# Two encoder layers on one core: where the second layer's weight sums are issued

## The chip, the cores and the metric

The kernel runs on one core of one Trainium2 chip. That core has a matrix engine (TensorE, PE in the profile; its weight loads are shown apart as PEld), three engines for element-wise work (VectorE is DVE, ScalarE is ACT, GpSimd is POOL), a queue that issues transfers (SyncE, SP) and 16 DMA engines, which move data between the chip's memory (DRAM) and the core's own. The metric is the time of one execution in microseconds (us), and the number given is the median of several runs. One further execution was recorded by the hardware profiler, and everything said of single instructions is from that one.

## The reference, cut to what matters

Two layers run over 512 tokens of width 1024, all in 32-bit floats. Each layer has a mixer (neighbourhood attention beside grouped-query attention, GQA), an attention over 256 memory tokens, and a feed-forward part:

```python
def conv_ffn(h, w_up, conv_w, conv_b, w_down):
    u = h @ w_up                                   # 512 x 1024 by 1024 x 5632
    up = jnp.pad(u, ((0, 0), (1, 1), (0, 0)))
    u = up[:, :-2] * conv_w[0] + up[:, 1:-1] * conv_w[1] + up[:, 2:] * conv_w[2] + conv_b
    gate, val = jnp.split(u, 2, axis=-1)
    return (jax.nn.silu(gate) * val) @ w_down      # 512 x 2816 by 2816 x 1024

for l in range(DEPTH):                             # DEPTH = 2
    x = x + hybrid_mixer(rms_norm(x, norm_mix[l]), w_in[l], ...)
    x = x + memory_cross_attention(rms_norm(x, norm_mem_q[l]), rms_norm(mem, norm_mem_kv[l]), ...)
    x = x + conv_ffn(rms_norm(x, norm_ffn[l]), w_up[l], conv_w[l], conv_b[l], w_down[l])
return rms_norm(x, norm_final)
```

## The kernel before, in words

The activations stand with the width on the 128 partitions, in 8 pieces of 128 x 512 (`xT`). The feed-forward width of 2816 is worked off in 22 columns of 128, `j` = 0 to 21, and for each column there is a gate half and a value half of the product with `w_up`.

**Weight sums.** Columns 0 to 3 (`PLAIN = 4`) are plain products (`up`). From column 4 on (`up_forms`, line 1975) the kernel cuts tokens, input width and gate/value into halves, and gets the eight half products of a column from seven, in the manner of Strassen and Winograd. Those seven need sums of weight blocks: from the four quarters of a `w_up` column (a11, a12 of the gate side, a21, a22 of the value side) the kernel makes two tensors in DRAM, `dr_sums` and `dr_diffs`. It makes them with transfers alone, no engine of the core adds anything. `make_form` (line 717) makes one half of one such tensor in two transfers: SP copies a quarter of `w_up` from DRAM to DRAM (shown as line 80), and then a transfer issued by POOL (line 731) adds a second quarter, or a sum made before, onto it. One call of `make_form` is called **a form** here. The columns 4 to 21 come in four shares (`SHARES_OF_FORMS`: columns 4 to 7, 8 to 11, 12 to 16, 17 to 21), each share needs four forms, so there are 16 forms in a layer. The transfers of a form carry 1024 KB each in the first two shares and 1280 KB in the last two.

The forms of both layers stand in one list, `form_queue`, the first layer's 16 ahead of the second layer's 16. Each call takes the next one from the list. The calls stand in the program at fixed places, the same in each layer:

- six in the GQA sweep (line 1737, at every third of its steps),
- four in the memory attention (line 1853),
- eleven in the feed-forward part (line 2173, at each even column: 0, 2, 4, ... 20).

That makes 21 places in a layer for 16 forms. `make_form(upto=DEPTH)` has an argument: it does nothing when the next form in the list belongs to a layer that is not below `upto`. In the kernel before, all three places call it without an argument.

**How the sums are read.** In the order of `sequence()` (line 848) each column from 4 on asks for four weight tiles, `gate`, `val` (of the column before), `sums` and `diffs`, and for tiles of `w_down` in between. SP loads each into one of five buffers named `raw` (`emit_raw`), ACT rounds it to `hi` (line 801), POOL, or DVE for the `sums`, subtracts to get the rest `lo` (line 802), and PE multiplies with both (line 103). After each product the partial results in the PSUM banks (`mm`, `sc`, `tr`) are put together by DVE, ACT and POOL (lines 2002 to 2051), and a bank is free for PE's next product only when that is done.

**What sets the order.** SP works strictly in the order in which the program is written: a load and a form's copy stand in one queue, and a load whose `raw` buffer is not yet free holds all that stands behind it. The order on PE, ACT, DVE and POOL comes from a planner in the kernel (`class Order`, line 359 on). It replays the whole program with a cost for each instruction and a model of the transfers, in 12 rounds with random draws, and keeps the best order that it finds. So a change to SP's queue can also move instructions on the other engines, even ahead of the place that was edited.

Of the kernel before, what the change touches and what calls it, by code (L numbers as in the profile page):

```python
# [695 lines left out]
def encoder_kernel(ctx: ExitStack, tc: tile.TileContext, t: dict, out: bass.AP):  # L696
# [20 lines left out]
    def make_form(upto=DEPTH):  # L717


        if not form_queue or form_queue[0][0] >= upto:  # L720
            return
        l, g, n = form_queue.pop(0)
        j, nj = SHARES_OF_FORMS[g]
        w, half = t["w_up"][l], D // 2
        gate, val = slice(P * j, P * (j + nj)), slice(D_FF + P * j, D_FF + P * (j + nj))
        sums, diffs = made[l][g]
        a11, a12, a21, a22 = w[:half, gate], w[half:, gate], w[:half, val], w[half:, val]
        dst, base, more = [(sums[:half], a21, a22), (sums[half:], a11, sums[:half]),
                           (diffs[half:], a11, a21), (diffs[:half], a12, sums[half:])][n]
        SP.dma_start(dst, base)  # L730
        nc.gpsimd.dma_start(dst, more, accum_op=ALU.add, max_dma_last_dim=4 * P * nj)
# [486 lines left out]
    for l in range(DEPTH):  # L1218
# [672 lines left out]
        def up(j):  # L1891
            up_finish(j, [up_project(j, side) for side in range(2)])
# [73 lines left out]
        def split_form(name, where=None):  # L1966


            place = xform[name] = [rtile((2, S)) for _ in range(2)] if where is None else [where[:, :2], where[:, 2:]]
            direct = {"b11": (0, 0), "b21": (1, 0), "b22": (1, 1)}  # L1970
            for i in range(len(place)):
                src = quarter(*direct[name])[i] if name in direct else raw_forms[name][:, 2 * i : 2 * i + 2]
                halves_of(name, i, src, name == "t4", POOL if name == "b22" else DVE)
# [81 lines left out]
        def down(g, rows):  # L2055
            j0, nj = GROUPS[g]
            ops = [acts[j] for j in range(j0, j0 + nj)]
            for m in rows:
                pm = ps_mm()
                gemm_T(pm, get_w(("down", g, m)), ops, range(nj), 0, nj - 1)  # L2060
                DVE.tensor_add(xT[m], xT[m], pm)
# [106 lines left out]
        for what, n, rows in sequence():  # L2168
            if what == "down":
                down(n, rows)  # L2170
                continue
            if what in ("up", "gate") and n % 2 == 0:
                make_form()
            if what == "gate":
                open_units[n] = up_forms(n)
            if what != "up":
                next(open_units[n])
                continue
            if n == 0:
                up_first()  # L2180
                token_sums()
            elif n > 1:
                up(n)
                if n == PLAIN - 1:
                    split_form("t3", ffn.hi[:, :4])
                    split_form("b22", ffn.lo[:, :4])
                    split_form("t4", ffn.hi[:, 4:])
# [92 lines left out]
```

## Time and profile before

| what | value |
|---|---|
| median of 3 runs | 1301.23 us (1299.8 to 1301.89) |
| the profiled execution: its time, its span | 1299.96 us, 1298.2 us |
| PE busy | 1286.4 us, 99% of the span |
| PEld, DVE, ACT, POOL busy | 84%, 71%, 61%, 66% |
| granted TensorE clock | 0.998 |
| data moved by DMA | 241.22 MB, mean 186 GB/s |

The span is the time from the first to the last instruction, and 1.76 us of the execution's time lie outside of it. "Busy" is the share of the span in which an engine had an instruction in work; PE's instructions overlap each other, so its busy time says that PE was hardly ever left without work, and not that it worked at its peak. In the rows of a timeline the columns are the start in us, the duration in us, the engine, the line of the program, the operation, what it writes and reads, and in square brackets how long the engine had been idle and who released it. In the rows of a tile the three numbers behind the count are the least, the median and the greatest duration in ns, and the two behind them the first and the last start in us. A row of DMA issues gives the count, the size of one transfer and the median us from issue to landing. In the rows of windows each engine has its busy us in that stretch and its number of instructions, and at the end stand the granted clock, the share of the time that the 16 DMA engines were busy, and GB/s.

### The profile page before, as it was taken

How to read it: one execution, taken by the hardware profiler on the slowest of the kernel's cores; microseconds unless marked ns; L12 is line 12 of the kernel's file. 1: busy time of each engine (PE TensorE's matmuls, PEld its weight loads, DVE VectorE, ACT ScalarE, POOL GpSimd, SP SyncE). 2: the span in 40 equal slices, each digit the busy share in tenths (PEclk: the TensorE clock that was granted, in tenths of full speed). 3: DMA queues.
4: the chain of work that ended last, by engine and by line, in shares of the span. 5: the costliest groups of instructions: out<-in, count | busy, mean ns of one | idle time of the engine just before them, and what ended most of it. 6: DMA issues, size and time to landing. Idle time of an engine off the chain costs nothing.

```text
span 1298.2 us, 19571 instructions
## 1 busy us (share of the span) xinstructions
PE 1286.4 (99%) x6731; PEld 1094.9 (84%) x6731; DVE 916.4 (71%) x1727; ACT 787.4 (61%) x1487; POOL 861.3 (66%) x656
## 2 busy tenths in 40 slices
PE   9999999999999999999999999999999999999997
PEld 8888888888888888888888888888888888888887
DVE  6558877668976765866635597776789767667565
ACT  6667867566554654554636678765656556456444
POOL 3657967727767776776746569767376776667663
PEclk9999999999999999999999999999999999999999
DMA  9734499596989898797455435998974555555541
GB/s 290 208 107 126 150 258 208 165 249 190 235 219 250 220 260 219 215 245 204 147 152 174 141 76 168 266 213 251 217 188 124 164 157 158 163 154 155 145 134 65
DMA packets 293699, 241.22 MB, mean 186 GB/s; under 512 B 7777, under 2 KB 249953, under 8 KB 293601
## 3 DMA queue, kind: packets, MB, share of 16 engines
q1 hardware_dynamic: 276288, 201.83, 52.4%
q0 software_dynamic: 16896, 37.75, 16.2%
q8 instruction: 53, 0.87, 0.3%
q10 hardware_dynamic: 416, 0.39, 0.1%
q14 instruction: 46, 0.37, 0.1%
HBM read 229.99 MB, written 77.59 MB: 237 GB/s over the span
## 4 chain that ended last, share of the span: by engine, by line
PE 94%; DVE 3%; ACT 1%; issue 1%; POOL 0%; POOLq 0%; ACTq 0%; DVEq 0%
PE mm L103 68%; PE sc L103 18%; PE tr L103 5%; PE tr L1606 2%; PE tr L1451 1%; PE tr L1800 1%; DVE sc L1423 0%; DVE r L1317 0%; DVE r L1100 0%; DVE t L1509 0%; ACT hi L801 0%; DVE r L1149 0%; PE tr L1521 0%; ACT t L1429 0%; DVE t L1476 0%
## 5 line engine op out<-in xcount | busy, mean ns | idle before, releaser
L802 POOL TENSOR_TENSOR lo<-raw,hi 128x512 fp32r<-128x512 f32 (+3 forms) x329 | 575.9, 1770 | 254.3 <-ACT hi L801 209.7
L801 ACT CAST hi<-raw 128x1024 fp32r<-128x1024 f32 (+2 forms) x369 | 295.0, 815 | 280.5 <-issue 60.1
L103 PE MATMUL mm<-r,hi 128*128 128x512 f32 (+1 forms) x1376 | 419.2, 389 | 0.0
L103 PEld LDWEIGHTS mm<-r,hi 128*128 128x128 f32 x1376 | 249.3, 188 | 43.8
L103 PE MATMUL mm<-r,lo 128*128 128x512 f32 (+1 forms) x864 | 261.4, 344 | 0.0
L103 PE MATMUL mm<-xg,hi 128*128 128x512 f32 x768 | 227.5, 392 | 1.3 <-DVE sc L2046 1.3
L103 PEld LDWEIGHTS mm<-r,lo 128*128 128x128 f32 x864 | 152.1, 188 | 26.8 <-DVE lo L802 1.7
L103 PEld LDWEIGHTS mm<-xg,hi 128*128 128x128 f32 x768 | 140.6, 188 | 28.1 <-ACT t L2031 1.5
L103 PE MATMUL mm<-xg,lo 128*128 128x256 f32 (+1 forms) x528 | 139.7, 331 | 0.0
L103 PE MATMUL mm<-hi,xg 128*128 128x512 f32 (+1 forms) x384 | 111.1, 359 | 0.0
L103 PEld LDWEIGHTS mm<-xg,lo 128*128 128x128 f32 x528 | 89.2, 188 | 15.4
L1106 POOL TENSOR_SCALAR t<-t,s 128x512 f32<-128x512 f32 (+1 forms) x112 | 67.7, 627 | 45.7 <-DVE s L1590 23.0
L103 PE MATMUL sc<-xg,hi 128*128 128x512 f32 x304 | 89.4, 395 | 0.0
L2044 POOL TENSOR_TENSOR t<-t 128x256 f32<-128x256 f32 x36 | 43.6, 1211 | 68.4 <-ACT t L2043 68.4
L103 PEld LDWEIGHTS mm<-hi,xg 128*128 128x128 f32 x384 | 68.0, 189 | 9.1 <-DVE r L1300 0.2
L802 DVE TENSOR_TENSOR lo<-raw,hi 128x1024 fp32r<-128x1024 f32 (+1 forms) x40 | 54.0, 1350 | 30.6 <-ACT hi L801 30.6
L103 PE MATMUL sc<-r,r 128*128 128x256 f32 (+1 forms) x352 | 73.9, 330 | 0.0
L103 PE MATMUL mm<-lo,xg 128*128 128x512 f32 (+1 forms) x192 | 68.5, 357 | 0.0
L1099 ACT CAST r<-tr 128x512 fp32r<-128x512 f32 x79 | 45.6, 587 | 36.4 <-DVE tr L1914 25.6
L2051 DVE TENSOR_TENSOR sc<-mm,t 128x256 f32<-128x256 f32 x36 | 15.6, 432 | 71.3 <-ACT t L2050 71.3
L103 PEld LDWEIGHTS sc<-xg,hi 128*128 128x128 f32 x304 | 55.6, 191 | 10.4 <-ACT xg L80 0.4
L1100 DVE TENSOR_TENSOR r<-tr,r 128x512 fp32r<-128x512 f32 x79 | 53.4, 685 | 12.4 <-ACT r L1099 8.8
(232 smaller groups left out, 2389.6 us busy)
## 6 DMA issues: line engine op xcount, KB each, us to landing
raw<-in_w_up SPq DMA_DIRECT2D x52, 512.0 KB, 4.8
raw<-dr_sums SPq DMA_DIRECT2D x36, 512.0 KB, 4.1
raw<-dr_diffs SPq DMA_DIRECT2D x36, 512.0 KB, 4.7
raw<-in_w_in SPq DMA_DIRECT2D x25, 512.0 KB, 5.0
raw<-in_w_down SPq DMA_DIRECT2D x32, 384.0 KB, 4.4
dr_sums<-in_w_up SPq DMA_DIRECT2D x8, 1280.0 KB, 9.9
dr_diffs<-in_w_up SPq DMA_DIRECT2D x8, 1280.0 KB, 9.2
raw<-in_w_up SPq DMA_DIRECT2D x36, 256.0 KB, 3.5
```

The source lines that it names most:

```text
L103: return self.engine.matmul(out, lhsT, rhs, **k)
L801: act.copy(hi[:, k], raw[:, k])
L802: (POOL if eng[0] == "P" else DVE).tensor_sub(lo[:, k], raw[:, k], f(hi)[:, k])
L1099: ACT.copy(hi, ps)
L1100: DVE.tensor_sub(lo, ps, f(hi))
L1106: eng.tensor_scalar(e, e, sums[:, col : col + 1], 1.0, op0=ALU.mult, op1=ALU.mult)
L1451: PE.transpose(tr[:, (2 * i + c) * P : (2 * i + c + 1) * P], es[j][:, i, c * P : (c + 1) * P], ident)
L1606: PE.transpose(tr[:, k * P : (k + 1) * P], es[j][:, k * P : (k + 1) * P], ident)
L1800: PE.transpose(tr[:, (2 * c + i) * P : (2 * c + i + 1) * P], e[:, i, c * P : (c + 1) * P], ident)
L2044: POOL.tensor_add(vc, vc, u2)
L2051: DVE.tensor_add(ch, ah, l4)
```

## The change

```diff
@@ -2170,7 +2170,7 @@
                 down(n, rows)
                 continue
             if what in ("up", "gate") and n % 2 == 0:
-                make_form()
+                make_form(l + 1)
             if what == "gate":
                 open_units[n] = up_forms(n)
             if what != "up":
```

`make_form` itself is as it was:

```python
    def make_form(upto=DEPTH):
        if not form_queue or form_queue[0][0] >= upto:
            return
        l, g, n = form_queue.pop(0)
        ...
        SP.dma_start(dst, base)
        nc.gpsimd.dma_start(dst, more, accum_op=ALU.add, max_dma_last_dim=4 * P * nj)
```

Only the calls in the feed-forward part are touched. In the first layer (`l` = 0) they now stop when the first layer's 16 forms are through. Ten of these are issued in the GQA sweep and the memory attention, six at the columns 0 to 10, and the calls at the columns 12 to 20 do nothing; before, those five issued the first five forms of the second layer. In the second layer the forms then begin with the first one of the layer: six in the GQA sweep, four in the memory attention, six at the columns 0 to 10. Before, the second layer had eleven forms left, and one of them fell into its feed-forward part. The number of transfers and of bytes over the whole program is the same.

SP's queue in the first layer's feed-forward part, at column 12. `dr_sums_86` is the second layer's first share (the number is the tile's), `raw` are the buffers into which weights are loaded. Before:

```order
L80 DMA raw_4918<-dr_diffs_83 128x8x128
L80 DMA raw_4946<-in_w_down 128x6x128
L80 DMA dr_sums_86<-in_w_up 512x512
L80 DMA raw_4979<-in_w_up 128x8x128
L80 DMA raw_5005<-in_w_up 128x4x128
L80 DMA raw_5035<-dr_sums_82 128x8x128
```

Now:

```order
L80 DMA raw_4918<-dr_diffs_83 128x8x128
L80 DMA raw_4946<-in_w_down 128x6x128
L80 DMA raw_4977<-in_w_up 128x8x128
L80 DMA raw_5003<-in_w_up 128x4x128
L80 DMA raw_5033<-dr_sums_82 128x8x128
```

The form's copy has gone from between the loads, and the loads stand in the order in which they stood.

SP's queue in the second layer's feed-forward part, at column 6. `dr_sums_86` is read here; `dr_sums_92` is the last share of the second layer, which is read from column 17 on. Before:

```order
L80 DMA raw_10512<-dr_sums_86 128x8x128
L80 DMA raw_10542<-in_w_down 128x5x128
L80 DMA raw_10566<-dr_diffs_87 128x8x128
L80 DMA raw_10594<-in_w_down 128x5x128
L80 DMA raw_10622<-in_w_up 128x8x128
L80 DMA raw_10648<-in_w_up 128x4x128
L80 DMA raw_10678<-dr_sums_86 128x8x128
```

Now:

```order
L80 DMA raw_10506<-dr_sums_86 128x8x128
L80 DMA raw_10536<-in_w_down 128x5x128
L80 DMA raw_10560<-dr_diffs_87 128x8x128
L80 DMA raw_10588<-in_w_down 128x5x128
L80 DMA dr_sums_92<-in_w_up 512x640
L80 DMA raw_10618<-in_w_up 128x8x128
L80 DMA raw_10644<-in_w_up 128x4x128
L80 DMA raw_10674<-dr_sums_86 128x8x128
```

A copy of 1280 KB now stands ahead of the next column's two loads of `w_up`; five more stand likewise at the columns 0, 2, 4, 8 and 10 (the one at column 0 was there before, with another form).

POOL's order at the same place of the second layer's feed-forward part (lines 2032 and 2044 are the putting together of a product's parts, line 802 makes `lo`). Before:

```order
L2032 TENSOR_TENSOR t_10479<-t_10479 128x256
L802 TENSOR_TENSOR lo_10563<-raw_10453,hi_10562 128x1024
L802 TENSOR_TENSOR lo_10591<-raw_10486,hi_10590 128x512
L2044 TENSOR_TENSOR t_10480<-t_10480 128x256
L802 TENSOR_TENSOR lo_10645<-raw_10542,hi_10644 128x640
```

Now:

```order
L2032 TENSOR_TENSOR t_10473<-t_10473 128x256
L802 TENSOR_TENSOR lo_10585<-raw_10480,hi_10584 128x512
L731 DMA dr_sums_92<-in_w_up 512x640
L2044 TENSOR_TENSOR t_10474<-t_10474 128x256
L802 TENSOR_TENSOR lo_10641<-raw_10536,hi_10640 128x640
```

The accumulating transfer of a form now stands ahead of the instruction of line 2044, which is part of freeing a PSUM bank, and one `lo` stands elsewhere.

## The prediction

> **What bounds the kernel now.** I read the page first, then who PE waited for, then the stretches of the program side by side, then the one place where PE stood still in a feed-forward part.
>
> ```profile
> span 1298.2 us, 19571 instructions
> PE 1286.4 (99%) x6731; PEld 1094.9 (84%) x6731; DVE 916.4 (71%) x1727; ACT 787.4 (61%) x1487; POOL 861.3 (66%) x656
> PE 94%; DVE 3%; ACT 1%; issue 1%; POOL 0%; POOLq 0%; ACTq 0%; DVEq 0%
> ```
>
> PE is busy for 1286.4 of 1298.2 us, and 94% of the chain that ended last is PE. The change takes no product away and adds none, so the time can only move through PE's gaps. These are PE's waits between 100 and 1270 us, all of them:
>
> ```profile
> PE mm L103 <- DVE sc L2046: 1.3, 1, 1.3
> PE tr L1521 <- DVE r L1100: 0.8, 1, 0.8
> PE tr L1451 <- DVE r L1317: 0.8, 1, 0.8
> PE tr L1606 <- DVE r L1317: 0.4, 1, 0.4
> PE mm L103 <- POOL lo L802: 0.3, 1, 0.3
> PE mm L103 <- DVE t L1477: 0.2, 1, 0.2
> ```
>
> Together 3.8 us, each happened once, and none is put down to a transfer. Now the stretches (the columns are PE, PEld, DVE, ACT, POOL busy us, clock, DMA share, GB/s):
>
> ```profile
> 300.00:455.00 155.00, 153.65 (x783) 130.47 (x782) 123.29 (x187) 88.87 (x138) 111.87 (x68) 1.00 0.89 229
> 455.00:610.00 155.00, 155.00 (x805) 132.23 (x804) 100.18 (x161) 79.89 (x122) 113.17 (x72) 1.00 0.88 228
> 640.00:785.00 145.00, 143.93 (x788) 123.42 (x787) 91.18 (x218) 92.03 (x218) 89.20 (x90) 1.00 0.47 139
> 785.00:945.00 160.00, 159.64 (x823) 134.01 (x822) 117.80 (x251) 108.96 (x223) 107.63 (x93) 1.00 0.88 229
> 945.00:1090.00 145.00, 145.00 (x742) 123.52 (x741) 115.00 (x175) 82.76 (x128) 99.33 (x61) 1.00 0.56 149
> 1090.00:1275.00 185.00, 185.00 (x968) 157.99 (x967) 122.36 (x199) 95.37 (x148) 125.94 (x76) 1.00 0.51 146
> ```
>
> The first two rows are the first layer's feed-forward part, whose first half holds six forms of its own layer and whose second half holds the five that the change removes. The last two rows are the same part of the second layer, now with one form, then with six. The DMA engines are busy for 0.88 of the time beside forms and for 0.56 or less without. Where the five forms lie now, PE is busy for 155.00 of 155.00 us: there is no gap to win. In the first half it lost 1.35 us, and that is the price of a form at its worst. How it came about, in order of time:
>
> ```profile
> 366.58 0.53 SPq L80 DMA_DIRECT2D dr_sums<-in_w_up  x1
> 368.01 1.01 POOL L731 DMA_DIRECT2D dr_sums<-in_w_up  x1
> 368.11 7.61 SPq L80 DMA_DIRECT2D raw<-in_w_up  x2
> 377.92 4.46 SPq L80 DMA_DIRECT2D raw<-in_w_down  x1
> 383.23 1.05 ACT L801 CAST hi<-raw 128x1024 fp32r<-128x1024 f32 x1 [6.39 <-DMA raw<-in_w_up]
> 388.67 1.73 POOL L2044 TENSOR_TENSOR t<-t 128x256 f32<-128x256 f32 x1
> 390.44 0.43 DVE L2045 TENSOR_TENSOR tr<-sc,t 128x256 f32<-128x256 f32 x1 [0.63 <-POOL t L2044]
> 391.49 0.71 PE L103 MATMUL mm<-xg,hi 128*128 128x512 f32 x2 [1.35 <-DVE sc L2046]
> ```
>
> SP issues a form's copy, POOL issues the accumulating transfer, and the weight loads that stand behind the copy are late: ACT, which works in order, stands for 6.39 us until a tile of `w_up` has landed. What ACT, POOL and DVE then do to free the bank comes late, and PE waits 1.35 us. So a form costs time by way of late weights, and only when the delay outlasts what has been prepared ahead. How much that is, the waits of ACT for weights say, the first three rows for 300 to 455 us and the other two for 455 to 610 us (total, times, longest):
>
> ```profile
> ACT hi L801 <- DMA raw<-in_w_up: 6.4, 1, 6.4
> ACT hi L801 <- DMA raw<-dr_sums: 4.1, 2, 2.1
> ACT hi L801 <- DMA raw<-dr_diffs: 2.0, 1, 2.0
> ACT hi L801 <- DMA raw<-in_w_up: 8.8, 3, 4.9
> ACT hi L801 <- DMA raw<-dr_sums: 1.0, 1, 1.0
> ```
>
> Waits up to 4.9 us reached PE in no case (the second stretch has no gap), the one of 6.4 us with 1.35. About 5 us are covered: 6.39 - 1.35 = 5.04.
>
> **The change part by part.** First the dates of the forms. The rows give the copies and the reads of `dr_sums`: the first layer's first copies and reads, the three of the five moved forms that write `dr_sums`, then the second layer's copies and reads.
>
> ```profile
> L80 SPq DMA_DIRECT2D dr_sums<-in_w_up x6: 582/600/1497, 142.5 to 260.9; - x6
> L80 SPq DMA_DIRECT2D raw<-dr_sums x8: 366/367/2016, 319.2 to 435.3; - x8
> L80 SPq DMA_DIRECT2D dr_sums<-in_w_up x3: 1084/1867/3123, 455.7 to 579.9; - x3
> L80 SPq DMA_DIRECT2D dr_sums<-in_w_up x5: 582/610/720, 785.7 to 899.7; - x5
> L80 SPq DMA_DIRECT2D raw<-dr_sums x18: 366/366/367, 960.3 to 1229.5; - x18
> ```
>
> *The first read.* The second layer's first form went out at 455.7 us and is read from 960.3 us on, 504.6 us later. It will go out in the slot that now begins at 785.7 us, 174.6 us ahead of the read. In the first layer the distance is 319.2 - 142.5 = 176.7 us, with the same forms at the same places, and PE waits there for nothing of the kind. Cost: 0, covered by the whole attention; if it weren't, every us of lateness would be a us of PE. The Trainium skill speaks against the change here: "DMA: Bandwidth & Descriptors", section "Rules for kernel authors", tells one to issue a transfer early and to wait for it late, and by that the longer lead of before is the better one. By these rows the shorter lead is ample too, so by the rule and by the row the sum gets 0 from it.
>
> *The first layer's feed-forward part, 455 to 610 us.* Five copies on SP and five accumulating issues on POOL go. PE has no gap there, so 0. The most that could be hidden in PE's overlapping rows: 155.00 us for 805 products are 192.5 ns each, against 185.00/968 = 191.1 ns in the second layer's stretch without forms. That is 1.4 ns x 805 = 1.1 us, and the two stretches do not hold quite the same mix, so the bounds are -1.1 and 0; I take 0, since waits for weights of up to 4.9 us did not reach PE.
>
> *The second layer's attention, 640 to 945 us.* Six forms stand in the GQA sweep and four in the memory attention before and after. Only which ones changes: six of 1024 KB in place of three of 1024 and three of 1280, then two and two in place of four of 1280. Less to move, and little of it: 768 KB and 512 KB less in the copies, and as much in the accumulating ones. The planner swaps some neighbouring instructions here, by order alone. PE's gaps in this stretch are 1.07 + 0.36 = 1.43 us; they may vanish or double. Bounds -1.4 and +1.4, I take 0, there being no reason for either sign.
>
> *The second layer's feed-forward part, 945 to 1090 us.* It gets six copies of 1280 KB where it had one. This is the one place where the change adds load ahead of something that is needed soon. How the loads fare there now, and how with six forms (the first layer, 300 to 455 us), is in these rows; the first two are of the first layer, the others of the second one (945 to 1275 us), with the issue's duration in ns and the us to landing:
>
> ```profile
> L80 SPq DMA_DIRECT2D raw<-in_w_down x10: 367/373/4465, 347.1 to 451.8; - x10
> DMA to landing us min/median/max: 2.8/6.5/15.0
> L80 SPq DMA_DIRECT2D raw<-in_w_down x31: 328/368/535, 988.1 to 1257.9; - x31
> DMA to landing us min/median/max: 2.6/3.8/8.3
> ```
>
> With forms beside it an issue of a load took up to 4.465 us instead of 0.535, and landing up to 15.0 us, 6.5 in the middle, instead of 8.3 and 3.8. So the loads of columns 4 to 11 will land some 2.7 us later than now, which the 5.0 us of cover hold, and now and then by 6 us or more, which they don't. What stands behind such a load on ACT is the rounding of the later tiles and the copies that free PE's banks, and PE waits for those. Price of one such case: 1.35 us. How many: the first layer's feed-forward part has eleven forms (six and then five) and one case, so six forms should bring 6/11 of one, 0.74 us. The bounds are 0 (all covered, as were the last five) and 6 x 1.35 = 8.1 us (each form brings one). I take 0.74, being nearest to the row with the same forms.
>
> *POOL.* Each accumulating issue costs POOL about 1.01 us (the row at 368.01), and one stands right ahead of line 2044 on which a bank's release hangs. Five more of them make 5.1 us in a stretch in which POOL is idle for 145.00 - 99.33 = 45.7 us. 0, and at most 5.1 us if each fell on PE; that end lies inside the 8.1 above.
>
> **The sum.** Against the profiled execution: 1299.96 + 0 + 0 + 0.74 + 0 = 1300.7 us. The median of the runs lies 1301.23 - 1299.96 = 1.27 us above that execution, so the forecast for the median is 1301.97, rounded 1302.0 us: no change that can be told, with a lean to slower. 0.2%, 2.6 us, is about what a measurement of this kernel can tell from no change, so "same" reaches from 1298.6 to 1303.8.
>
> **The rivals.**
>
> *All covered.* No stall arises in the second layer, as none arose beside the last five forms of the first: 1301.2 us. For it speaks that ten of eleven forms cost PE nothing; against it that the very arrangement that cost 1.35 us comes again, the same form ahead of the same column.
>
> *Each form holds up the loads behind it: slower.* The place is SP's queue at columns 0 to 10 of the second layer, the price 1.35 us a form, and it decides as soon as the delay passes 5.0 us. Two stalls make 2.7 us and 1303.9, which is already slower; all six make 8.1 us and 1309.3. For it: the issues of up to 4.465 us and the landing of 15.0. Against it: of eleven such forms, one did. The Trainium skill's "DMA: Bandwidth & Descriptors", section "Queues, rings and completion order", says that each DMA engine takes what one queue gave it in ring order. By that rule a load behind a copy on SP's queue always waits for it, which is this rival; the trace agrees only in part, since most loads behind a copy were in time.
>
> *Less load in the first layer pays: faster.* The hidden 1.1 us come back, and the 1.43 us of gaps in the second layer's attention close by the new order: 2.5 us, 1298.7, just short of what can be told. It needs all of both. The gap of 1.35 us in the first layer can't help, since the forms go only from 455.7 us on.
>
> *The second layer's sums come too late.* If a form of columns 12 to 21 were read before it is made, PE would stand until it is there; 10 us would give 1311. Against it: the first layer makes the same forms in the same slots and its PE waits for none.
>
> **How the numbers follow.** The forecast, none to one stall and small swaps, has 0.52; all covered 0.18; held-up loads 0.20; faster 0.07; too late 0.03. Same: 0.52 + 0.18 = 0.70. Slower: 0.20 + 0.03 = 0.23. Faster: 0.07. The range begins at 1302.0 - 1.1 - 1.4, about 1299.5, and ends with three stalls at 1301.23 + 4.05, about 1305.3. The likeliest case by itself reaches from 1300.0 to 1303.8.
>
> **What would show it.** In the profile after, the stretch from 455 to 610 us has a DMA share near 0.56 instead of 0.88, and PE's busy time there stays whole. The stretch from 945 to 1090 us has a share near 0.88, issues of loads beyond 1 us, and waits of ACT for `raw`, of which there are none now. A PE wait behind line 2046 or its like near 1030 us would be the stall forecast; its length is the term. ACT waits beyond 5 us without a stall, or stalls behind shorter ones, would make the cover wrong. Waits of SP for `dr_sums` in the second layer would be the last rival. PE gaps in the second layer's attention other than 1.4 us would be the planner's doing, and a gap anywhere ahead of 455 us would be too. Most of all the forecast would be wrong if the median moved by more than 2.6 us without new PE waits: then PE's overlapping rows hide more than I think.

## The result and the profile after

The changed kernel took 1303.6 us in the median of 14 runs (1302.35 to 1305.57), and the kernel before, run beside it, 1300.44 us (14 runs, 1299.34 to 1303.18). The ratio is 1.0024 with a 95% interval of 1.0017 to 1.0031: slower by 0.24%, 3.2 us, just past the 0.2% that the prediction took as what can be told from no change. The time lies inside the range of the prediction and 1.6 us above its number.

The profiled execution took 1304.16 us against 1299.96 us before. First its page: span and engines.

```profile
span 1302.4 us, 19579 instructions
PE 1286.9 (99%) x6731; PEld 1094.5 (84%) x6731; DVE 922.4 (71%) x1727; ACT 787.0 (60%) x1487; POOL 861.2 (66%) x656
```

PE was busy for 1286.9 us as against 1286.4: the products cost nearly what they cost before, and 3.7 of the 4.2 us of the longer span are time in which PE stood. PE's waits between 100 and 1270 us after the change (total, times, longest):

```profile
PE mm L103 <- DVE sc L2046: 2.5, 2, 1.3
PE tr L1521 <- DVE r L1100: 1.2, 2, 0.8
PE tr L103 <- DVE r L1100: 1.1, 1, 1.1
PE mm L103 <- DVE xg L1100: 1.1, 1, 1.1
PE tr L1451 <- DVE r L1317: 0.8, 1, 0.8
PE mm L103 <- POOL lo L802: 0.3, 1, 0.3
PE mm L103 <- DVE t L1477: 0.2, 1, 0.2
```

7.2 us where there were 3.8. The first row has a second wait, the third and the fourth row are new, and each of the three is between 1.1 and 1.3 us long. Where they lie is in the stretches after the change (PE, PEld, DVE, ACT, POOL busy us, clock, DMA share, GB/s):

```profile
300.00:455.00 155.00, 153.71 (x783) 130.54 (x782) 123.65 (x188) 88.60 (x138) 111.96 (x69) 1.00 0.88 229
455.00:610.00 155.00, 155.00 (x806) 132.27 (x805) 100.18 (x161) 80.28 (x123) 108.30 (x66) 1.00 0.60 162
640.00:785.00 145.00, 143.53 (x786) 123.23 (x785) 92.19 (x217) 92.04 (x218) 88.75 (x89) 1.00 0.47 138
785.00:945.00 160.00, 158.64 (x818) 132.82 (x817) 119.05 (x250) 107.44 (x221) 105.90 (x91) 1.00 0.82 211
945.00:1090.00 145.00, 143.56 (x729) 121.75 (x727) 114.20 (x172) 80.84 (x126) 101.00 (x63) 1.00 0.92 232
1090.00:1275.00 185.00, 184.07 (x948) 156.66 (x949) 124.56 (x199) 96.87 (x149) 129.29 (x79) 1.00 0.56 154
```

The first layer's feed-forward part is as it was: the forms of 455 to 610 us are gone (DMA share 0.88 to 0.60), and PE, which had no gap there, won nothing. The second layer's feed-forward part, the last two rows, lost 145.00 - 143.56 + 185.00 - 184.07 = 2.37 us. The second layer's attention lost 0.40 us in its first half and 159.64 - 158.64 = 1.00 us in its second. Together that is 3.8 us, about all that PE lost.

**The first new wait, at 1032 us,** in the timeline after the change. It is at column 6 of the second layer, and its rows are those of the wait at 390 us one layer earlier:

```profile
1008.95 0.53 SPq L80 DMA_DIRECT2D dr_sums<-in_w_up  x1
1010.39 0.98 POOL L731 DMA_DIRECT2D dr_sums<-in_w_up  x1
1010.48 6.57 SPq L80 DMA_DIRECT2D raw<-in_w_up  x2
1025.41 1.05 ACT L801 CAST hi<-raw 128x1024 fp32r<-128x1024 f32 x1 [5.93 <-DMA raw<-in_w_up]
1030.85 1.73 POOL L2044 TENSOR_TENSOR t<-t 128x256 f32<-128x256 f32 x1
1032.61 0.43 DVE L2045 TENSOR_TENSOR tr<-sc,t 128x256 f32<-128x256 f32 x1 [0.63 <-POOL t L2044]
1033.66 0.70 PE L103 MATMUL mm<-xg,hi 128*128 128x512 f32 x2 [1.20 <-DVE sc L2046]
```

Copy, accumulating transfer, two loads of `w_up` (the 6.57 us of their row reach from the first issue to the end of the second; each took 0.37 us), ACT standing for 5.93 us until the first of them has landed, and POOL and DVE late behind it; PE then stood for 1.20 us. The two transfers are not of one form: the copy is column 6's, and the accumulating transfer is that of the form at column 4, whose copy went out at 979 us. A form's own can only go out once its copy has landed, and here POOL came to it just as SP sent the next copy.

**The second one, at 1089 us,** stands behind the form of column 10. The timeline after the change:

```profile
1063.42 1.00 POOL L731 DMA_DIRECT2D dr_diffs<-in_w_up  x1
1073.23 4.92 SPq L80 DMA_DIRECT2D dr_diffs<-in_w_up  x1
1078.91 1.06 ACT L801 CAST hi<-raw 128x1024 fp32r<-128x1024 f32 x1 [2.61 <-DMA raw<-dr_diffs]
1087.20 1.05 ACT L801 CAST hi<-raw 128x1024 fp32r<-128x1024 f32 x1 [3.31 <-DMA raw<-dr_sums]
1090.88 1.20 PE L103 MATMUL tr<-r,hi 128*128 128x512 f32 x4 [1.12 <-DVE r L1100]
```

Here no wait of ACT was above 3.4 us, but two came within 8.3 us, and PE stood for 1.12 us. The issue of column 10's copy itself took 4.92 us; 9.8 us ahead of it the accumulating transfer of the form before had gone out, and it landed 14.3 us after its issue.

**The third, at 862 us,** lies in the memory attention, where nothing was edited. The timeline after the change, and behind it the rows of the kernel before at the same place:

```profile
859.02 1.02 POOL L731 DMA_DIRECT2D dr_diffs<-dr_sums  x1
859.73 2.87 POOL L802 TENSOR_TENSOR lo<-raw,hi 128x512 fp32r<-128x512 f32 x2
860.16 2.74 DVE L1702 TENSOR_TENSOR mm<-t,mem_rep 128x256 f32<-128x256 f32 x1
862.82 0.68 DVE L1100 TENSOR_TENSOR xg<-tr,xg 128x512 fp32r<-128x512 f32 x1
863.55 0.74 PE L103 MATMUL mm<-xg,r 128*128 128x512 f32 x2 [1.10 <-DVE xg L1100]
```

```profile
859.94 2.72 POOL L802 TENSOR_TENSOR lo<-raw,hi 128x512 fp32r<-128x512 f32 x2
860.35 1.17 DVE L1702 TENSOR_TENSOR mm<-t,mem_rep 128x256 f32<-128x256 f32 x1
862.60 1.04 POOL L731 DMA_DIRECT2D dr_diffs<-in_w_up  x1
```

Before, the issue of the form stood behind the two `lo`; now the planner has put it ahead of them. DVE's instruction of line 1702 beside them took 2.74 us in place of 1.17, ending with the second `lo` and not with the first, and DVE's `xg`, for which PE waits, is late by that.

The loads of `w_down` and ACT's waits for weights in the second layer's feed-forward part, after the change (count, then least, median and greatest issue in ns, first and last start; us to landing, of all loads into `raw` there; ACT's waits in total, times, longest):

```profile
L80 SPq DMA_DIRECT2D raw<-in_w_down x12: 368/373/3727, 989.4 to 1109.1; - x12
DMA to landing us min/median/max: 2.8/7.3/15.5
ACT hi L801 <- DMA raw<-in_w_up: 5.9, 1, 5.9
ACT hi L801 <- DMA raw<-dr_sums: 4.2, 2, 3.3
ACT hi L801 <- DMA raw<-dr_diffs: 2.6, 1, 2.6
```

Issues of up to 3.727 us and landing after 7.3 us in the middle; the kernel before had no wait of ACT for weights here.

### The profile page after: what moved, and what is told of

Same layout as the page of the kernel before. It is cut to its first block, busy times and chain, and to the rows that moved or that the text cites. A ratio compares the mean times of both kernels' runs of the same rounds, so it can differ in the third digit from the quotient of the medians.

```text
span 1302.4 us, 19579 instructions
## 1 busy us (share of the span) xinstructions
PE 1286.9 (99%) x6731; PEld 1094.5 (84%) x6731; DVE 922.4 (71%) x1727; ACT 787.0 (60%) x1487; POOL 861.2 (66%) x656
## 4 chain that ended last, share of the span: by engine, by line
PE 91%; DVE 4%; ACT 2%; issue 1%; DMA 1%; POOL 0%; SPq 0%; POOLq 0%; ACTq 0%; DVEq 0%
PE mm L103 66%; PE sc L103 17%; PE tr L103 5%; PE tr L1606 2%; PE tr L1451 1%; DMA raw<-dr_sums 1%; PE tr L1800 1%; DVE r L1149 1%; SPq L80 0%; ACT hi L801 0%; DVE r L1100 0%; DVE sc L1423 0%; DVE r L1317 0%; DVE s L1581 0%; DVE t L1509 0%
## 5 line engine op out<-in xcount | busy, mean ns | idle before, releaser
L1584 ACT ACTIVATE t<-sc,s,qr 128x512 f32<-128x512 f32 x64 | 49.3, 776 | 22.1 <-DVE s L1106 21.9
```

The lines of the kernel that those rows point to most:

```text
L1584: ACT.activation(e, sc[j], AF.Exp, bias=nmx[:, c], scale=qrs[b][:, col : col + 1], accum_out=sums[:, c])
```

## The experiments

The first theory was that the six forms of the second layer's feed-forward part make the weights late, and the third wait is the planner's doing. Three things were open: whether the loads are late because they stand behind the copy in SP's queue, or because copy and accumulating transfer use the same DMA engines; whether the order that the planner draws makes the whole difference; and what makes two forms of six cost something and four nothing. Each run was timed beside the kernel before on the same chip, and the ratio is to that. It is worked out over the runs and need not be the quotient of the two medians.

| edit | kernel before, median us | this, median us | ratio, 95% interval |
|---|---|---|---|
| three forms stay in the first layer | 1302.01 | 1301.64 | 0.9998 (0.9985 to 1.001) |
| last six copies issued by POOL | 1302.01 | 1314.79 | 1.0098 (1.008 to 1.0115) |
| last six forms without their accumulating transfer | 1302.01 | 1301.79 | 0.9999 (0.9988 to 1.0009) |
| other draws of the planner, after | 1302.01 | 1305.26 | 1.0027 (1.0015 to 1.0039) |
| fourth form of the second layer without its accumulating transfer | 1301.59 | 1303.28 | 1.0016 (1.0007 to 1.0025) |
| before, no form at column 6 | 1301.59 | 1300.52 | 0.9991 (0.9983 to 1.0) |
| one form stays in the first layer | 1301.59 | 1300.96 | 1.0003 (0.9993 to 1.0014) |
| after, no form at column 6 | 1300.57 | 1305.12 | 1.0028 (1.0015 to 1.004) |
| before, forms spread, three in the first layer and three in the second | 1300.57 | 1297.7 | 0.9972 (0.9961 to 0.9983) |
| other draws of the planner, before | 1300.57 | 1303.22 | 1.0012 (1.0002 to 1.0022) |
| after, forms spread | 1301.62 | 1299.67 | 0.9984 (0.9975 to 0.9992) |
| before, forms spread, one in the first layer and five in the second | 1301.62 | 1298.62 | 0.9979 (0.997 to 0.9989) |

Each kernel was profiled once, and the executions of one kernel differ: those of the kernel before took 1299.38 to 1306.42 us in the 29 runs of the first rows. Part of that is PE's clock. In the profile of "after, no form at column 6" it was this, ahead of and behind PE's wait of 2.73 us (columns as in the stretches above):

```profile
1123.00:1127.30 4.30, 1.57 (x9) 1.22 (x8) 4.27 (x5) 1.32 (x2) 4.30 (x4) 1.00 0.65 152
1127.40:1130.80 3.40, 3.40 (x12) 2.82 (x11) 1.18 (x4) 2.00 (x4) 1.96 (x2) 0.50 1.06 192
```

For 3.4 us the granted clock was 0.50, which costs some 1.7 us on top of the wait (an estimate, half of 3.4). In the fourteen profiles this followed five of the eight waits of PE of 1.9 us and more between 300 and 1275 us, and none of the shorter ones there. And in those 29 runs of the kernel before, 15 executions with a mean clock of 0.999 took 1300.7 us on average, 8 with 0.998 took 1302.3 and 6 with 0.997 took 1304.0. So a long wait can cost more than its length, and a median also holds how often that happens.

### Half of the change: three forms stay

```diff
-                make_form(l + 1)
+                make_form(DEPTH if n <= 16 else l + 1)
```

> The first layer's feed-forward part keeps three of the five forms of the second layer (columns 12, 14, 16); the second layer's feed-forward part then has forms at columns 0, 2 and 4 alone. Theory A (a form's transfers hold up the weight loads of the second layer's feed-forward part, and two of the six outlast what is prepared ahead, those at columns 6 and 10): both gaps of PE near 1032 and 1089 us are gone, PE is busy for all of 945 to 1090 us, and the time is some 2.6 us under the changed kernel's, about 1301 us. Theory B (the planner's new order, not the forms, makes the gaps): PE's gaps have about the same sum as in the changed kernel, 4 us more than before, at whatever place, and the time stays near 1303.6 us.

All new waits went, in the attention too (159.79 busy of 160.00 us), and the time is that of the kernel before. The profile is of the shortest of this kernel's 12 executions, 1298.97 us. The second layer's stretch in this run:

```profile
945.00:1090.00 145.00, 145.00 (x740) 123.24 (x739) 115.65 (x173) 82.78 (x129) 100.29 (x61) 1.00 0.67 180
```

Three forms at the columns 0, 2 and 4 cost PE nothing; the loss hangs on what the forms at 6, 8 and 10 do, and on the order in the attention.

### Which part of a form makes the loads late

The copies of the last six forms go to POOL's queue, so that nothing but loads is left in SP's:

```diff
-        SP.dma_start(dst, base)
+        if l == 1 and 4 * g + n >= 10:
+            InOrder(tc, nc.gpsimd, kept).dma_start(dst, base)
+        else:
+            SP.dma_start(dst, base)
```

> As the changed kernel, but the copies of the last six forms of the second layer are issued by POOL instead of SP: the same bytes at about the same time, in another queue than the weight loads. Theory A1 (the loads are late because they stand behind a copy in SP's queue): SP's issues of loads stay under 0.6 us in the second layer's feed-forward part, ACT no longer waits for raw there by more than 1 us, both gaps of PE are gone, some 2.6 us less, about 1301 us. Theory A2 (the loads are late because the 16 DMA engines are shared, by whatever queue): ACT still waits for raw by 3 us and more, and gaps of 1 us and more remain in that part; the time stays at 1302.5 to 1304.

The loads are as late as with the copies between them. Loads of `w_up` and ACT's waits in this run:

```profile
L80 SPq DMA_DIRECT2D raw<-in_w_up x19: 367/368/4920, 946.6 to 1109.9; - x19
DMA to landing us min/median/max: 2.9/6.0/16.5
ACT hi L804 <- DMA raw<-dr_sums: 7.1, 1, 7.1
ACT hi L804 <- DMA raw<-in_w_down: 6.3, 1, 6.3
```

An issue of a load still took up to 4.920 us though no copy stood ahead of it in its queue. So the order in SP's queue alone is not what delays the loads. The time was far above the 1302.5 to 1304 expected. PE waited for 3.0 and 2.9 us in the second layer's feed-forward part, and its clock stood at 0.50 for 3.4 us in the first layer and for 6.8 us in the second. POOL issues six more transfers here, and the planner gave PE another order at some places; what share each of these has is not shown.

The last six forms without their accumulating transfer (the sums of the columns 12 to 21 of the second layer lack one term):

```diff
-        nc.gpsimd.dma_start(dst, more, accum_op=ALU.add, max_dma_last_dim=4 * P * nj)
+        if l == 0 or 4 * g + n < 10:
+            nc.gpsimd.dma_start(dst, more, accum_op=ALU.add, max_dma_last_dim=4 * P * nj)
```

> As the changed kernel, but the last six forms of the second layer leave out their accumulating transfer, so the sums of the columns 12 to 21 lack a term there; the copies on SP stay. Theory A1 (SP's queue, by the copies): SP's issues of up to 4.9 us and at least one of the two gaps near 1032 and 1089 us stay. Theory A2 (the shared DMA engines): half of the forms' bytes are gone, landings fall from 15 us to under 9 us, both gaps go, some 2.6 us less, about 1301 us.

The stretch in this run:

```profile
945.00:1090.00 145.00, 145.00 (x740) 123.45 (x739) 114.93 (x176) 82.72 (x127) 97.70 (x60) 1.00 0.64 186
```

With the copies still between the loads no issue took more than 0.54 us and PE has no gap. The attention's wait of 1.1 us stayed, as it should. The two runs together: copies alone, behind which the loads stand, cost PE nothing, and copies with accumulating transfers cost something from whichever queue the copies come. Leaving out the accumulating transfers also halves what the forms move, so these two runs alone don't tell the kind of transfer from the amount.

No run leaves out the copies alone, but the traces show what an accumulating transfer does by itself. In the changed kernel the copy of column 6 landed at 1016.0 us, and the accumulating transfer of 1010.39 us landed at 1024.9. This is what the DMA engines moved between 1017.5 and 1022 us (packets, MB, share of the 16 engines; q0 holds POOL's transfers and q1 SP's):

```profile
q0 software_dynamic: 281, 0.72, 85.7%
q1 hardware_dynamic: 282, 0.14, 16.5%
```

There were as many packets of the loads as of the accumulating transfer, but the latter's are five times as large, so the loads got a sixth of the engines' time. The two loads of `w_up` issued at 1010.48 and 1016.68 us landed at 1025.3 and 1026.2 us, right behind it; with no transfer of a form in flight a load of this profile landed after 3.9 us in the middle. In the last but one kernel below (the change with spread forms) an accumulating transfer went out at 1060.73 us, when the last copy had landed 14 us before. Between 1064 and 1069 us all 351 packets were its own, though SP had issued loads at 1065.1 and 1066.7 us. In the feed-forward parts of all fourteen profiles SP issued 530 loads more than 0.2 us behind an accumulating transfer that had not landed yet, and each of the 530 landed behind it. A copy holds the loads back too, only for less long: of 150 loads issued behind a copy, with no accumulating transfer in flight, 149 landed behind it, but they did so within 10.2 us, against up to 15.3 us behind an accumulating transfer. So the accumulating transfer is the part of a form that makes the loads so late, by taking most of the DMA engines' time.

### The planner's part

```diff
-ROUNDS, REPLAYS, MARGIN, SHARES, STRETCH, SEED = 12, 4, 100.0, (0.0, 0.0, 0.5, 1.0, 2.0), 500, 4
+ROUNDS, REPLAYS, MARGIN, SHARES, STRETCH, SEED = 12, 4, 100.0, (0.0, 0.0, 0.5, 1.0, 2.0), 500, 5
```

On the changed kernel:

> The changed kernel with another seed for the planner's random draws (5 for 4): the same work and the same queue on SP, another order of neighbouring instructions on the other engines. Theory A: the two gaps near 1032 and 1089 us stay (2.6 us together), and only the gap of 1.1 us near 863 us, in the attention, may go or move: 1302 to 1304 us. Theory B: the gaps of the feed-forward part go or move too, and the time changes by 2 us or more either way.

On the kernel before:

> The kernel before with another seed for the planner's draws (5 for 4). If the planner's draws alone move the time by as much as the change did, it differs from before by 2 us or more either way. If the gaps come from the places of the forms, which are the same here, the time stays within 1 us of before and the gap near 390 us stays.

With other draws the changed kernel keeps the wait at column 6 (2.1 us) and the one in the attention (1.1 us), and the one at 1089 us is gone. Its time, 1305.26 us, is above the 1302 to 1304 expected: in the profile the wait at 390 us was 2.1 us long, with the clock at 0.50 for 3.4 us behind it. The kernel before with the same draws lost 1.6 us by the ratio (1.0012) and 2.6 us by the medians, more than the 1 us that was expected, by new waits of 0.5 to 1 us in the first layer. So the draws alone move the time by half or more of what the change does. With the new draws the changed kernel is still the slower of the two (1.0027 and 1.0012), but the intervals overlap, and the two were timed on different chips: how much of the change's 0.24% is luck of the draw is not settled by the times. The wait at column 6 of the second layer came with both draws.

The wait in the attention, taken by itself (the fourth form of the second layer without its accumulating transfer; half of `dr_diffs` of the columns 4 to 7 lacks a term):

```diff
-        nc.gpsimd.dma_start(dst, more, accum_op=ALU.add, max_dma_last_dim=4 * P * nj)
+        if (l, g, n) != (1, 0, 3):
+            nc.gpsimd.dma_start(dst, more, accum_op=ALU.add, max_dma_last_dim=4 * P * nj)
```

> As the changed kernel, but the accumulating transfer of the second layer's fourth form is left out (half of dr_diffs of the columns 4 to 7 lacks a term). In the changed kernel POOL issues it at 859.0 us right ahead of two lo of line 802, and the DVE instruction of line 1702 beside them takes 2.74 us, against 1.17 in the kernel before, where no issue stands ahead of the pair. If that order makes the gap of 1.1 us at 863 us: line 1702 falls to about 1.2 us there, the gap goes, the stretch 785 to 945 us is busy for 159.6 or more of 160.0 us, and the time falls by 1.1 us, to some 1302.5, the two gaps of the feed-forward part staying. If the gap comes from elsewhere (the lighter or heavier transfers, the order on PE), line 1702 stays at 2.7 us and the gap stays.

The same place in the timeline of this run (lines one higher), and the stretch:

```profile
860.00 2.72 POOL L803 TENSOR_TENSOR lo<-raw,hi 128x512 fp32r<-128x512 f32 x2 [0.47 <-ACT hi L802]
860.63 0.95 DVE L1703 TENSOR_TENSOR mm<-t,mem_rep 128x256 f32<-128x256 f32 x1
785.00:945.00 160.00, 159.86 (x825) 134.12 (x824) 117.89 (x252) 108.76 (x224) 106.41 (x92) 1.00 0.78 205
```

Beside the same two `lo`, without the issue ahead of them, DVE took 0.95 us, and PE's wait is gone. The mechanism is shown. The time was 1303.28 us, not some 1302.5, but the kernel before was longer too beside this run: by the ratios, 1.0016 against the change's 1.0024, about 1 us was won as expected, though the intervals overlap. In this execution the waits in the feed-forward parts were 2.0 us at 390, 1.8 us at 1032 and 0.5 us at 1089. In all fourteen profiles it is the same: in the seven in which the issue stands right ahead of the pair of `lo`, line 1702 took 2.7 to 2.9 us and PE waits there for 1.1 to 1.3 us; in the other seven it took 0.9 to 1.4 us and PE does not wait.

### Which forms cost something

The kernel before without a form at column 6:

```diff
-            if what in ("up", "gate") and n % 2 == 0:
+            if what in ("up", "gate") and n % 2 == 0 and n != 6:
                 make_form()
```

> The kernel before, without a call at column 6 in either layer: the first layer's feed-forward part issues ten forms in place of eleven, the second layer's two in place of one. If the forms that stand close together at columns 4 and 6 (a copy and an accumulating transfer at once) make the first layer's gap of 1.35 us at 390 us, it goes, and the time is 1.3 us under the kernel before, 0.1%, near 1299 to 1300; this would be the fastest version. If any form of that part can make such a gap, it comes at another column and the time stays.

The wait at 390 us went, so it hangs on the form of column 6: in the nine profiles with that form in the first layer PE waited there for 1.0 to 2.1 us, and in the five without it not at all. A smaller wait came at column 12 (0.7 us at 478 us) and the planner's wait in the attention came too, and the gain was 0.09%.

The changed kernel with one form left in the first layer, so that the second layer's columns 0 to 8 have one each:

```diff
-                make_form(l + 1)
+                make_form(DEPTH if n <= 12 else l + 1)
```

> The first layer's feed-forward part keeps one of the five forms (column 12); the second layer's then has forms at columns 0, 2, 4, 6 and 8. If a gap belongs to the form of its column: the gap near 1032 us (column 6) stays with 1.2 us or more, the one near 1089 us (column 10) is gone, and the time lies between the kernel with three left and the changed one, 1.3 us over the former. If only the sum of forms counts, gaps lie at any column.

A miss: the form at column 6 is there, and PE's wait at 1032 us was under 0.1 us. In this run the accumulating transfer of the form before was issued 4 us ahead of that column's copy (1005.9 and 1009.9 us), and not 1.4 us behind it as in the changed kernel.

The changed kernel without column 6, the forms one place later:

```diff
-            if what in ("up", "gate") and n % 2 == 0:
+            if what in ("up", "gate") and n % 2 == 0 and n != 6:
                 make_form(l + 1)
```

> The changed kernel without a call at column 6: in both layers the six forms of the feed-forward part stand at columns 0, 2, 4, 8, 10 and 12. If the gaps come where a copy is issued within 1.5 us of an accumulating transfer (columns 4 and 6), the gaps near 390 and 1032 us go, and smaller ones of about 0.9 us may come at column 12, as they did without column 6 before; the gap of 1.1 us at 863 us in the attention stays, since POOL's order there is that of the changed kernel. Time: 2 us under the changed kernel, about 1301.5. If any form costs the same wherever it stands, 1303.6 stays.

A clear miss: 1305.12 us where 1301.5 were expected. The profile is of the longest of the 11 executions, 1309.05 us. The waits at 390 and 1032 us went, and longer ones came at column 12's form, 2.1 us at 479 and 2.7 us at 1124, each with the clock at 0.50 for 3.4 us behind it. There a copy and the accumulating transfer of the form before were issued 2.4 to 3.5 us apart, and some 23 us behind the copy before. So column 6 as such is not to blame; at the waits of the columns 6, 10 and 12 alike, transfers of two forms overlapped.

Spread wider, with fewer such overlaps, the forms should cost nothing. The kernel before with nine places instead of eleven in each feed-forward part, three or four columns between some:

```diff
-            if what in ("up", "gate") and n % 2 == 0:
+            if what in ("up", "gate") and n in (0, 2, 4, 8, 11, 13, 16, 18, 20):
                 make_form()
```

> The kernel before with the calls of the feed-forward part at columns 0, 2, 4, 8, 11, 13, 16, 18 and 20: the first layer issues three of the second layer's forms there, the second layer three of its own, at columns 0, 2 and 4. If wide distances between forms avoid the gaps and the second layer's attention is that of the kernel with three forms left (no gap at 863 us), no gap of 1 us and more is left between 130 and 1270 us: 1299 to 1300, 1.5 to 2 us under the kernel before, the fastest version. If the gaps come by chance of the order, one or two of about 1 us appear elsewhere and the time equals that of before.

The best of all, and better than the 1299 to 1300 expected: 1297.7 us, 0.28% faster than the kernel before (0.9972, 0.9961 to 0.9983), where the changed kernel stands at 1.0024. PE's waits between 100 and 1270 us in this run:

```profile
PE tr L1451 <- DVE r L1317: 0.8, 1, 0.8
PE mm L103 <- DVE t L1477: 0.6, 2, 0.4
PE mm L103 <- POOL lo L802: 0.3, 1, 0.3
PE tr L1606 <- DVE r L1317: 0.2, 1, 0.2
```

1.9 us in all, and none in a feed-forward part.

The change itself with spread forms, all six still in the second layer's feed-forward part:

```diff
-            if what in ("up", "gate") and n % 2 == 0:
+            if what in ("up", "gate") and n in (0, 2, 4, 8, 11, 13):
                 make_form(l + 1)
```

> The changed kernel (each layer issues its own sums alone) with the six forms of the feed-forward part at columns 0, 2, 4, 8, 11 and 13 in both layers. If the change's loss is the place of the forms in the second layer's feed-forward part plus POOL's order in its attention, then with these columns PE has no gap of 0.9 us and more in the feed-forward part of either layer, the gap of 1.1 us at about 862 us stays, with 2.7 us for the DVE instruction of line 1702, and the time is some 1.2 us over the spread kernel with three forms left (1297.7): 1298.5 to 1299.5, under the kernel before. If issuing six forms in the second layer's feed-forward part costs as such, gaps remain near 1032 or 1089 us and the time is 1301 or more.

The second layer's stretch and ACT's waits for weights in this run:

```profile
945.00:1090.00 145.00, 145.00 (x742) 123.55 (x741) 117.21 (x175) 82.87 (x128) 102.37 (x64) 1.00 0.82 212
ACT hi L801 <- DMA raw<-in_w_up: 7.8, 3, 4.1
```

Six forms, a DMA share of 0.82, three waits of ACT of up to 4.1 us, and PE loses nothing. Of the waits that the change brought only those in the attention are left (the planner's 1.1 us, and 0.4 us at 774 us), and the time, 1299.67 us, is 0.2 us above what was expected. So it is not the number of forms in the second layer that cost the 2.4 us, but where they stand. That it is their distance is not shown: what is loaded beside the forms was not held the same.

The kernel before, spread, with one form of the second layer in the first and five in the second:

```diff
-            if what in ("up", "gate") and n % 2 == 0:
+            if what in ("up", "gate") and n in (0, 2, 4, 8, 11, 13, 18):
                 make_form()
```

> The same columns, and one form of the second layer in the first layer's feed-forward part (column 18), so that POOL has no issue ahead of the pair of lo near 860 us. If both causes are gone with that: no gap of 0.9 us and more between 130 and 1270 us, line 1702 at 0.9 to 1.4 us, the time within 1 us of the spread kernel with three left, 1297 to 1298.7. If five forms in the second layer's feed-forward part cost more than three, a gap is seen there and the time is 1299 or more.

1298.62 us: no wait of 0.9 us or more is left, and the planner did not put the issue ahead of the `lo` (line 1702: 1.36 us). Three spread kernels, with three, one and none of the second layer's forms in the first layer's feed-forward part, come to 0.9972, 0.9979 and 0.9984. The intervals overlap, and the last of the three has the planner's 1.1 us (0.08%) in it: once the forms are spread, the layer in which they stand hardly matters.

## Why the prediction was right or wrong

**The dates of the forms** were right: SP, which issues the reads, had no wait for a sum to be made in the second layer, and the first read, 176.5 us behind its form's copy, was in time. The rival of sums that come too late is out.

**The first layer's feed-forward part, 0 us,** was right: 155.00 busy of 155.00 us with a DMA share of 0.60 as with 0.88. The hidden 1.1 us of the lower bound did not come, and with them falls the rival "less load in the first layer pays".

**The second layer's attention, 0 us (bounds -1.4 to 1.4),** failed. The stretch lost 0.40 + 1.00 = 1.4 us, the upper bound. The step called the neighbouring swaps order alone and gave them no sign. One of the swaps put POOL's issue of 1.02 us ahead of two `lo`, and that held DVE's line 1702, and behind it PE for 1.10 us; the run without that issue shows it. The rest is small waits that moved, one of 0.43 us at 775 us among them. The swap could be read from the order beforehand, but its price could not: in the profile before, no issue stands right ahead of such a pair at this place.

**The second layer's feed-forward part, 0.74 us,** was right in its mechanism and too small. The wait forecast near 1030 us came at 1032 with 1.20 us, along the very chain shown for 390 us, with issues above 1 us (3.727), a late landing (7.3 us in the middle, 6.5 in the row taken from the first layer) and a DMA share of 0.92. But the count was the weak step: it took 6/11 of one stall, as if each place had the same chance. It was one place, column 6, and the same form comes at the same place again, so one whole stall, 1.35 us, was the nearer estimate; that the first layer's came in all nine profiles with that form bears this out. The second wait, at 1089 us, was not seen, because the cover was taken as 5.0 us for any single wait of ACT. It is not a fixed sum: 5.93 us cost 1.20 at column 6, and 2.61 and 3.31 us, 8.3 us apart, cost 1.12 at column 10, which fits a second delay that came before the first was made up for; this was not tried by itself. 2.37 us were measured in the place of 0.74.

**The rival "each form holds up the loads behind it"** came about in its mildest form: two stalls of six, 2.37 us, for which it gave 2.7. Its place was too narrow. The prediction put it into SP's queue, with the ring order of the Trainium skill's "DMA: Bandwidth & Descriptors", section "Queues, rings and completion order", beside it. What the section says of one queue's order agrees with the trace: in the thirteen profiles with the copies in SP's queue all 139 loads that stood behind a copy alone landed behind it. The prediction saw the trace agree only in part, since most such loads were in time; they were in time for PE, but none of them landed ahead of the copy. With the copies in another queue the loads were as late (issues of up to 4.920 us), and with the copies in SP's queue and no accumulating transfers they were in time for PE (no issue above 0.54 us). What decides is the accumulating transfer, which comes from POOL's queue and took 86% of the engines' time and more while it lasted.

**The other rule weighed,** to issue early and wait late, would have spoken against the change because of the shorter lead. The lead did nothing, as taken.

**The sum and the range.** Too small were the terms by 1.63 us in the feed-forward part and by 1.4 us in the attention. Against the medians, 3.2 us were to be explained and 0.74 were forecast. The likeliest case was "no change", with 0.70; what came was slower by 0.24%, a case given 0.23. The lean was right, and its size was not. In absolute time 1303.6 us even lies within the band that the prediction called "same", up to 1303.8, and here luck has a part: the sum began from 1301.23 us, a median of three runs, and the kernel before took 1300.44 us beside the change.

**What stays open.** An accumulating transfer delays the loads wherever it stands, and only some of them made PE wait; which ones isn't settled to a rule. An overlap with a copy does not tell. The two at the columns 6 and 12 that did were issued 1.4 to 3.5 us apart; but a pair 3.2 us apart in the kernel before (455.7 and 458.9 us) and three in the best kernel (0.2 to 3.1 us apart) cost nothing, nor did one 0.2 us apart at 1109.5 us in the changed kernel with spread forms. Nor does the distance to the copy before tell them apart: some 23 us at column 12 and 30 us at column 6 where it cost, 26 to 32 us in the best kernel where it didn't. Which loads fall beside the overlap, and how full the buffers are then, wasn't tried. The length of the wait at 390 us also differs between the profiles, 1.0 to 2.1 us, and with two seeds alone the part of the planner's draws in all these differences is not measured. Nor is it shown why the clock fell behind some long waits and not behind others. Nor is it shown why the planner swapped the issue with the `lo`, or why the issue makes DVE's instruction last over both of them.

## What to carry to other kernels

Where transfers in the background share the DMA engines with loads that are needed soon, ask what is loaded beside them before asking in which stage: the same six forms cost 2.4 us at the columns 0, 2, 4, 6, 8 and 10 and nothing at 0, 2, 4, 8, 11 and 13. Look at the packets of both: small ones that take turns with large ones get a small share. A cover measured at one stall holds for one late load; two that follow each other within some 8 us seem able to cost as much, though each lies below it (one case here). And where a planner sets the order, an edit in one stage can cost as much in another, so compare the orders there for instructions that now stand side by side.

## What the hardware showed that was not expected

A DVE instruction slows with what POOL does beside it. In the changed kernel line 1702 took 0.43 us at 857.10 us, where POOL stood idle, and 2.74 us beside two `lo`. The Trainium skill's "GPSIMD Engine Reference", section "1. Specifications", says that POOL's way into the on-chip memory is shared with VectorE and that instructions with two inputs from that memory contend for it; line 1702 has two, and the trace agrees. That it lasts over both `lo` when a transfer's issue stands ahead of them, and ends about with the first otherwise, is seen in all fourteen profiles.

Loads and an accumulating transfer moved packet for packet and not byte for byte, 282 against 281 packets with 0.14 against 0.72 MB in 4.5 us, so the loads were starved though the engines were busy throughout.

A transfer's issue can itself be held: a load of `w_up` that SP mostly issues in 0.37 us took up to 4.92 us while forms' transfers were in flight (the run with POOL's copies), and a form's copy, 0.53 us at column 6, took 4.92 us at column 10. It needs no copy: in the last kernel a load of `w_down` took 6.21 us to issue at 501 us, where an accumulating transfer was in flight and the last copy had landed 20 us before.
